# Splitting the raw pieces of each FFN's two ordinary pairs from buffers of their own, ahead of the turned tokens' copies

## The chip, the core and the metric

One NeuronCore of a Trainium2 chip runs the whole program. The metric is the device time of one execution in microseconds (us). A NeuronCore has a matrix engine (TensorE, PE in the profile, with its weight loads as PEld), a vector engine (VectorE, DVE), a scalar engine (ScalarE, ACT), a general engine (GpSimd, POOL) and a sync engine that issues transfers (SyncE, SP). PE accumulates into PSUM, which has 8 banks of 128x512 float32 here; the other engines read the banks and release them. Each engine works through its own list of instructions in order and waits at an instruction until what it needs is there.

## The reference

One layer of an encoder block on 512 tokens of width 1024: a half-step SwiGLU FFN, a token mixing stage, and a second half-step FFN, each between two RMS norms. The change touches the two FFNs:

```python
def _rmsnorm(x, g):
    xf = x.astype(jnp.float32)
    y = xf * lax.rsqrt(jnp.mean(xf * xf, axis=-1, keepdims=True) + NORM_EPS)
    return (y * g.astype(jnp.float32)).astype(x.dtype)

def _swiglu(x, w_gate, w_up, w_down):
    return (jax.nn.silu(x @ w_gate) * (x @ w_up)) @ w_down
...
    f = _swiglu(_rmsnorm(x, ffn1_pre_g[l]), ffn1_w_gate[l], ffn1_w_up[l], ffn1_w_down[l])
    x = x + 0.5 * _rmsnorm(f, ffn1_post_g[l])
...
    f = _swiglu(_rmsnorm(x, ffn2_pre_g[l]), ffn2_w_gate[l], ffn2_w_up[l], ffn2_w_down[l])
    x = x + 0.5 * _rmsnorm(f, ffn2_post_g[l])
```

D_MODEL is 1024 and D_FF is 2816, that is 22 blocks of 128 hidden features, each with a gate column block and an up column block.

## The kernel before

**Number format.** Every float32 operand of a product is split in two parts, `hi` (a rounded copy, made by ACT) and `lo` (what is left, made by DVE): `split`, lines 111 to 113. A product is then three matmuls, hi by hi, hi by lo, lo by hi (`mm3`, lines 190 to 193). So each weight piece of 128x1024 costs ACT one cast on line 112 and DVE one subtraction on line 113 before PE can use it.

**Weights.** They lie in DRAM in the order of use as pieces of 128x1024 (512 KB). `convert` (line 125) loads a piece into one of two `raw` buffers of the pool `wp` (SP, line 128) and splits it. Because there are only two such buffers, the load of the next piece waits on SP until DVE has finished the split that last read the buffer, and everything that stands behind that load on SP waits too. `fetch` converts the next piece.

**One FFN** (`ffn`, line 524) runs in these steps:

1. `first_products` (line 242): four early gate pieces, multiplied with the first 256 tokens. Between them PE transposes ("turns") the normed rows of token blocks 2 and 3 into the layout of the products: `turn_rows` calls `turned` (line 295), which puts four 128x128 transposes into a PSUM bank, twice for each token block; ACT copies the bank as `hn` hi (line 304), DVE makes the lo part (line 305). Each of the four early sums is copied to a unit `g` by ACT (line 262) and completed by DVE (line 263).
2. The turned banks of blocks 2 and 3 are kept, because after the early products `keep` (line 309) copies them once more as plain float32 into the units `whole` (eight ACT copies on line 312). With four banks for early sums and four kept ones, all 8 banks are taken until the first of these copies are done.
3. The first `STD` = 2 hidden blocks are done as ordinary pairs: `proj_into` of gate and of up, each 8 times three matmuls of 128x512. Their four pieces are numbers 4 to 7 of the FFN. Between them `combined` (line 314) builds on DVE and ACT the token combinations `sum` and `v` that the next step needs.
4. `seven` (line 399) does the other 20 pairs with seven products of 256 tokens in place of eight. Its weight blocks come from `load_blocks` (line 346): for a pair j below `EARLY` = 4 it loads four 128x512 tiles on SP (t1, t3, t4 and w11), and POOL then adds the gate or up half onto t1 and t3 by two accumulating transfers (lines 361 and 362). A pair from 4 on loads its gate piece into one of the same two `raw` buffers (line 358). The pairs 0 and 1 are loaded ahead (line 570), pair j + 2 when pair j begins (`get`). The products 5, 6, 3, 7 and 4 of the first four pairs need these blocks split, which ACT and DVE do in the order of use, among ACT's copies of results out of the banks (`up`, lines 441 and 449).
5. `down` then multiplies back to width 1024.

The tiles `x`, `raw` of the first pieces, `t1` to `t4`, `w11`, `whole`, `sum`, `v`, `g` and `h` are units of 128x512 from one pool of 54 (`up`, NUNIT), given out as they come free.

**What sets the order.** Within the marked stretches PE, ACT and DVE keep the order in which the program was written; elsewhere a scheduler at build time orders each engine's list. SP keeps the written order up to the end of FFN 1. In FFN 2 the SP list is the scheduler's. POOL keeps the written order in its marked stretches.

Of the kernel before, what the change touches and what calls it, by code (L numbers as in the profile page):

```python
# [13 lines left out]
F32R = mybir.dt.float32r  # L14
BF16 = mybir.dt.bfloat16
AF = mybir.ActivationFunctionType
# [4 lines left out]
P = 128  # L21
# [24 lines left out]
def block_kernel(ctx, tc, x, gains, weights, rpb_near, rpb_all, alibi0, alibi12, out):  # L46
# [13 lines left out]
    def unit(dt=F32, name="u"):  # L60
        return up.tile([P, 512], dt, tag="u", name=name)
# [52 lines left out]


    pieces = {}
    loads = deque()
    state = {"used": False, "next": 0, "take": 0, "stop": EARLY + 2 * STD, "ahead": lambda: None}
    ordered = []
# [2 lines left out]

    spread = {b + i for b in (3 * NF, total - 3 * NF) for i in range(SPREAD)}

    def convert(n, raw=None):
        if raw is None:
            raw = wp.tile([P, PIECE], F32, tag="raw", name="raw", bufs=2)
            nc.sync.dma_start(raw, weights[n])
        hi, lo = [wp.tile([P, PIECE], F32R, tag="w", name="w") for _ in range(2)]
        split(hi, lo, raw)  # L130
        pieces[n] = [[a[:, cs] for cs in halves] for a in (hi, lo)]
# [15 lines left out]
    def fetch():  # L147
        while state["next"] in pieces:
            state["next"] += 1
        if state["next"] < state["stop"]:  # L150
            convert(state["next"])
            state["next"] += 1
        else:
            state["ahead"]()
        for _ in range(2):
            if loads:
                loads.popleft()()
# [10 lines left out]
    def take(ahead=True):  # L168
        w = pieces.pop(state["take"])
        state["take"] += 1  # L170
        if ahead:
            fill(NPIECE - 1)
        return w
# [68 lines left out]
    def first_products(turns, early):  # L242

        w = [take(False) for _ in range(EARLY)]
        for i in range(EARLY):
            o = bank("q")
            for k0 in (0, 4):
                to = o[:, 64 * k0:64 * k0 + 256]
                parts = [cut(w[i], k * P, P) for k in range(k0, k0 + 4)]
                for j in range(4):  # L250
                    for part in parts[j]:
                        nc.tensor.matmul(to, part, hn_hi[:, k0 + j, 0:256], start=k0 + j == 0 and part is parts[j][0],
                                         stop=False, skip_group_check=True)
                for j in range(4):
                    nc.tensor.matmul(to, parts[j][0], hn_lo[:, k0 + j, 0:256], start=False, stop=j == 3,
                                     skip_group_check=True)
            if i in turns:
                turn_rows()
            if i == min(turns):
                fetch()  # L260
            g = unit(name="g")
            nc.scalar.copy(g[:, :256], o[:, :256])
            nc.vector.tensor_tensor(g[:, :256], g[:, :256], o[:, 256:], op=ALU.add)
            early.append((o, g))
        while kept:
            kept.popleft()()
        fetch()

    def sumsq(src, acc, f=1.0):

# [108 lines left out]
    def seven(use, mv, n_pairs, n0, behind, far, lead, raws, early):  # L379

        blocks = {}
        o = {}

        def get(j):
            if j < n_pairs and j not in raws:
                raws[j] = load_blocks(n0, j)  # L390
            elif j >= n_pairs:
                behind(far)

        def ready(j, i):
            if j < n_pairs:
                if j and loads:
                    loads.popleft()()
                if i == 1:
                    sums_of(raws[j])
                if j >= EARLY or i not in (1, 2):  # L400
                    blocks[j, i] = split_block(raws[j].pop(i))
            else:
                behind(lead)

        def product(j, i, key, start):
            if start:
                o[key, j] = bank(key)
            w = blocks.pop((j, i))
            acc = o[key, j][:, :256]
            for k in range(4):  # L410
                mm3(acc, w[:, k * P:(k + 1) * P], w[:, 512 + k * P:512 + (k + 1) * P], *mv[i][k],
                    start and k == 0, k == 3, skip_group_check=True)
            return acc

        res = {}
        get(0)
        get(1)
        for i in (1, 5, 2, 6, 3, 7, 4):
            ready(0, i)
        for j in range(n_pairs + 1):  # L420
            now, was = j < n_pairs, j > 0
            get(j + 2)
            if now:
                if j < EARLY:
                    o["q", j], g = early[j]
                    q = o["q", j][:, :256]
                else:
                    q = product(j, 1, "q", True)
                    g = unit(name="g")
                    nc.scalar.copy(g[:, :256], q)  # L430
                u = unit(name="up")
                res[j] = g, u
            ready(j + 1, 1)
            if was:
                q0 = product(j - 1, 7, "q", False)
                g0, u0 = res.pop(j - 1)
                nc.vector.tensor_tensor(u0[:, 256:], u0[:, 256:], q0, op=ALU.subtract)
            ready(j + 1, 5)
            if now:
                p = product(j, 5, "p", True)  # L440
                nc.scalar.copy(u[:, 256:], p)  # L441
            ready(j + 1, 2)
            if now and j >= EARLY:
                r = product(j, 2, "r", True)
                nc.vector.tensor_tensor(g[:, :256], g[:, :256], r, op=ALU.add)
            ready(j + 1, 6)
            if now:
                product(j, 6, "q", False)
                nc.scalar.copy(u[:, :256], q)
            ready(j + 1, 3)  # L450
            if was:
                product(j - 1, 4, "q", False)
                use(j - 1, g0, u0, q0)
            ready(j + 1, 7)
            if now:
                product(j, 3, "p", False)
                nc.vector.tensor_tensor(u[:, :256], p, u[:, :256], op=ALU.subtract)
            ready(j + 1, 4)
# [74 lines left out]
    def ffn(g, store, src):  # L533
        hidden = [None] * NF
        m = BLOCKS[store]
        feats = order_of(m)
        duos = [[None] * m for _ in range(2)]
        n0 = state["take"]

        def times(j, a, b):  # L540

            k = feats.index(j)
            if j < STD:
                hidden[k] = b
                nc.vector.tensor_tensor(b, a, b, op=ALU.mult)
                return
            for i in range(2):
                part = slice(i * 256, i * 256 + 256)
                if duos[i][k // 2] is None:
                    duos[i][k // 2] = unit(name="h")  # L550
                to = duos[i][k // 2][:, (k % 2) * 256:(k % 2) * 256 + 256]
                nc.vector.tensor_tensor(to, a[:, part], b[:, part], op=ALU.mult)

        def use(j, pg, pu):
            h = unit(name="h")
            nc.scalar.activation(h, pg, AF.Silu)
            times(j, pu, h)

        def use7(j, g, u, q):
            nc.scalar.activation(g[:, :256], g[:, :256], AF.Silu)  # L560
            nc.scalar.activation(g[:, 256:], q, AF.Silu)
            times(STD + j, u, g)

        raws = {}
        sums = combined()

        early = []
        first_products((0, 2) if store else (1, 2), early)
        mv = next(sums)
        for j in range(2):  # L570
            raws[j] = load_blocks(n0, j)
        for j in range(STD):
            ps = [bank(), bank()]
            for i in range(2):
                proj_into(ps[i], take(False))
                next(sums)
                if j < STD - 1:
                    fetch()
            use(j, *ps)
            if j == 0:  # L580
                ordered[-1].append(mark())
        g_post, g_pre = gain(g), None if store else gain(g + 1)
        if not store:
            bias_plan()
        after = n0 + 2 * NF
        state["stop"] = total if store else total - 3 * NF - NK

        far, lead, rest = down(m, after, duos, hidden, g_post, g_pre, store, src)
        state["next"] = state["take"] = after + 2 * m + 2
        seven(use7, mv, NF - STD, n0, lambda q: [f() for f in q.popleft()], far, lead, raws, early)  # L590
        rest()
# [1053 lines left out]
```

## Time and profile before

| | |
|---|---|
| median of three runs | 1096.55 us (1096.54 to 1097.75) |
| the profiled execution's own time | 1096.21 us |
| its span, first to last instruction | 1094.4 us |
| mean granted TensorE clock | 0.998 |
| PE idle, as far as a wait is named | 4.6, 3.5 (two waits), 1.2, 0.4 and 0.2 us |

The profile names an instruction by its line, engine, operation and the tiles it writes and reads; "idle before, releaser" says how long the engine stood before it and what ended that. The products of FFN 1 run to 346 us, those of the mixing stage from there to 747 us, those of FFN 2 from there to the end. A busy PE row is what the profile models as the matmul's own duration; the next matmul starts before it ends, so rates are read from start to start.

### The profile page before, as it was taken

How to read it: one execution, taken by the hardware profiler on the slowest of the kernel's cores; microseconds unless marked ns; L12 is line 12 of the kernel's file. 1: busy time of each engine (PE TensorE's matmuls, PEld its weight loads, DVE VectorE, ACT ScalarE, POOL GpSimd, SP SyncE). 2: the span in 40 equal slices, each digit the busy share in tenths (PEclk: the TensorE clock that was granted, in tenths of full speed). 3: DMA queues.
4: the chain of work that ended last, by engine and by line, in shares of the span. 5: the costliest groups of instructions: out<-in, count | busy, mean ns of one | idle time of the engine just before them, and what ended most of it. 6: DMA issues, size and time to landing. Idle time of an engine off the chain costs nothing.

```text
span 1094.4 us, 18389 instructions
## 1 busy us (share of the span) xinstructions
PE 1077.8 (98%) x6689; PEld 971.0 (89%) x6689; DVE 834.7 (76%) x1553; ACT 655.8 (60%) x1325; POOL 181.4 (17%) x252
## 2 busy tenths in 40 slices
PE   9999999999999999999999999999899999999997
PEld 7899999998888988888988888888799999998886
DVE  7988777778987778876477645776978777778985
ACT  6645655565784877667656641376455555565762
POOL 3212221014333000000000001142212111104301
PEclk9999999999999999999999999999999999999999
DMA  6999997569993454322132249552958777769962
GB/s 227 259 205 251 238 227 187 148 167 285 237 280 90 132 186 135 120 83 78 59 103 80 94 153 269 155 97 97 283 140 214 184 172 183 189 190 241 216 204 77
DMA packets 94573, 189.82 MB, mean 173 GB/s; under 512 B 23953, under 2 KB 26513, under 8 KB 94482
## 3 DMA queue, kind: packets, MB, share of 16 engines
q1 hardware_dynamic: 67168, 134.17, 36.9%
q0 software_dynamic: 24624, 54.01, 27.3%
q8 instruction: 52, 0.85, 0.3%
q10 hardware_dynamic: 2690, 0.46, 0.2%
q14 instruction: 39, 0.32, 0.1%
HBM read 183.58 MB, written 7.58 MB: 175 GB/s over the span
## 4 chain that ended last, share of the span: by engine, by line
PE 90%; DVE 4%; DMA 2%; ACT 2%; issue 1%; POOL 0%; SPq 0%; DVEq 0%; POOLq 0%; ACTq 0%
PE q L191 10%; PE q L193 10%; PE q L192 10%; PE ps L191 9%; PE ps L193 9%; PE ps L192 9%; PE p L191 3%; PE p L193 3%; PE p L192 3%; PE r L193 2%; PE r L192 2%; PE r L191 2%; PE c L192 2%; PE c L193 2%; PE c L191 2%; DVE w L113 1%
## 5 line engine op out<-in xcount | busy, mean ns | idle before, releaser
L113 DVE TENSOR_TENSOR w<-raw,w 128x1024 fp32r<-128x1024 f32 (+1 forms) x128 | 122.5, 957 | 76.2 <-ACT w L112 76.0
L112 ACT CAST w<-raw 128x1024 fp32r<-128x1024 f32 (+1 forms) x128 | 107.3, 839 | 88.6 <-PE ps L192 41.5
L191 PE MATMUL ps<-hn,w 128*128 128x512 f32 (+1 forms) x408 | 155.5, 381 | 3.5 <-ACT whole L312 3.5
L193 PE MATMUL ps<-hn,w 128*128 128x512 f32 (+1 forms) x408 | 153.6, 376 | 0.4 <-DVE w L113 0.2
L192 PE MATMUL ps<-hn,w 128*128 128x512 f32 (+1 forms) x408 | 153.1, 375 | 0.0
L112 ACT CAST w<-t 128x512 fp32r<-128x512 f32 x160 | 97.2, 619 | 54.5 <-DVE t L367 29.0
L113 DVE TENSOR_TENSOR w<-t,w 128x512 fp32r<-128x512 f32 x160 | 108.9, 689 | 25.8 <-ACT w L112 23.4
L191 PE MATMUL p<-v,w 128*128 128x256 f32 x320 | 90.9, 285 | 4.6 <-ACT up L441 4.6
L191 PEld LDWEIGHTS ps<-hn,w 128*128 128x128 f32 x408 | 76.9, 188 | 16.4 <-ACT whole L312 3.9
L192 PE MATMUL p<-v,w 128*128 128x256 f32 x320 | 90.9, 284 | 0.0
L191 PE MATMUL q<-v,w 128*128 128x256 f32 x320 | 90.8, 284 | 0.0
L193 PE MATMUL p<-v,w 128*128 128x256 f32 x320 | 90.8, 284 | 0.0
L192 PE MATMUL q<-v,w 128*128 128x256 f32 x320 | 90.8, 284 | 0.0
L193 PEld LDWEIGHTS ps<-hn,w 128*128 128x128 f32 x408 | 76.8, 188 | 15.6 <-DVE w L113 1.7
L193 PE MATMUL q<-v,w 128*128 128x256 f32 x320 | 90.6, 284 | 0.0
L192 PEld LDWEIGHTS ps<-hn,w 128*128 128x128 f32 x408 | 77.0, 189 | 12.5
L361 POOL DMA_DIRECT2D t<-in_weights_dram x40 | 35.0, 874 | 298.4 <-DMA t<-in_weights_dram 84.6
L193 PE MATMUL q<-hn,w 128*128 128x256 f32 x288 | 81.5, 283 | 0.0
L191 PE MATMUL q<-hn,w 128*128 128x256 f32 x288 | 81.5, 283 | 0.0
L192 PE MATMUL q<-hn,w 128*128 128x256 f32 x288 | 81.5, 283 | 0.0
L191 PE MATMUL q<-w,a 128*128 128x512 f32 x192 | 75.1, 391 | 0.4 <-DVE part L816 0.4
L192 PE MATMUL q<-w,a 128*128 128x512 f32 x192 | 74.7, 389 | 0.0
(268 smaller groups left out, 3023.3 us busy)
## 6 DMA issues: line engine op xcount, KB each, us to landing
raw<-in_weights_dram SPq DMA_DIRECT2D x98, 512.0 KB
t<-in_weights_dram SPq DMA_DIRECT2D x88, 256.0 KB
t<-in_weights_dram POOLq DMA_DIRECT2D x80, 256.0 KB, 5.7
w<-in_weights_dram SPq DMA_DIRECT2D x40, 256.0 KB
rows<-in_weights_dram SPq DMA_DIRECT2D x32, 256.0 KB
w<-in_weights_dram POOLq DMA_DIRECT2D x32, 256.0 KB, 6.1
tb<-in_weights_dram POOLq DMA_DIRECT2D x12, 512.0 KB, 8.4
rows<-in_weights_dram POOLq DMA_DIRECT2D x24, 256.0 KB, 10.8
```

The source lines that it names most:

```text
L112: nc.scalar.copy(hi, src)
L113: nc.vector.tensor_tensor(lo, src, hi.bitcast(F32), op=ALU.subtract)
L191: nc.tensor.matmul(o, sh, mh, start=start, stop=False, **kw)
L192: nc.tensor.matmul(o, sh, ml, start=False, stop=False, **kw)
L193: nc.tensor.matmul(o, sl, mh, start=False, stop=stop, **kw)
L361: nc.gpsimd.dma_start(t1, weights[gate][:, :512], accum_op=ALU.add)
```

## The change

The four pieces of the two ordinary pairs (4 to 7 of each FFN) no longer go through the two shared `raw` buffers. A new function `stage` gives each piece two units of its own and loads it as two halves of 128x512; `first_products` stages all four pieces of the FFN at its start. `convert` splits a staged piece half by half. `fetch` is called after each of the two turns (before: after the first turn, and after the `keep` copies), so the splits of the pieces 4 and 5 both stand ahead of the eight copies of line 312. `load_blocks` is called for three pairs ahead in place of two, and `get` leaves them out. In FFN 2 one small Silu activation on a 128x1 column, which brings its function table with it, is written ahead of the first products.

```diff
+    staged = {}
...
+    def stage(n):
+        staged[n] = [unit(name="raw"), unit(name="raw")]
+        for u, cs in zip(staged[n], halves):
+            nc.sync.dma_start(u, weights[n][:, cs])
+
     def convert(n, raw=None):
+        if n in staged:
+            hi, lo = [wp.tile([P, PIECE], F32R, tag="w", name="w") for _ in range(2)]
+            for u, cs in zip(staged.pop(n), halves):
+                split(hi[:, cs], lo[:, cs], u)
+            pieces[n] = [[a[:, cs] for cs in halves] for a in (hi, lo)]
+            return
         if raw is None:
...
     def first_products(turns, early):
 
         w = [take(False) for _ in range(EARLY)]
+        first = state["take"]
+        for n in range(first, first + 2 * STD):
+            stage(n)
...
             if i in turns:
                 turn_rows()
-            if i == min(turns):
                 fetch()
...
         while kept:
             kept.popleft()()
-        fetch()
...
         def get(j):
-            if j < n_pairs and j not in raws:
+            if j < n_pairs and j > 2:
                 raws[j] = load_blocks(n0, j)
...
         early = []
+        if store:
+            nc.scalar.activation(small("ms"), mhalf, AF.Silu)
         first_products((0, 2) if store else (1, 2), early)
         mv = next(sums)
-        for j in range(2):
+        for j in range(3):
             raws[j] = load_blocks(n0, j)
```

Two places show how instructions move. The first is SP's list in FFN 2, from the stores of the kept rows (`x_kept`) to the blocks of `seven`. Before (lines 128 and 358 are loads into the two shared buffers; t_8862 is the first tile of pair 2):

```order
L528 DMA x_kept<-x 128x512 x2
L128 DMA raw<-in_weights_dram 128x1024 x2
L350 DMA t_8660<-in_weights_dram 128x512
L351 DMA t_8661<-in_weights_dram 128x512
L355 DMA t_8664<-in_weights_dram 128x512
L360 DMA w_8659<-in_weights_dram 128x512
L350 DMA t_8670<-in_weights_dram 128x512
L351 DMA t_8671<-in_weights_dram 128x512
L355 DMA t_8674<-in_weights_dram 128x512
L360 DMA w_8669<-in_weights_dram 128x512
L358 DMA raw<-in_weights_dram 128x1024 x2
L350 DMA t_8862<-in_weights_dram 128x512
```

With the change, from the same place on (line 129 is `stage`, line 363 is `load_blocks`; t_8714 is the first tile of pair 2):

```order
L541 DMA x_kept<-x 128x512 x2
L129 DMA raw<-in_weights_dram 128x512 x2
L105 DMA gain_8885<-in_gains_dram 128x1024
L363 DMA t_8694<-in_weights_dram 128x512
L364 DMA t_8695<-in_weights_dram 128x512
L368 DMA t_8698<-in_weights_dram 128x512
L373 DMA w_8693<-in_weights_dram 128x512
L363 DMA t_8704<-in_weights_dram 128x512
L364 DMA t_8705<-in_weights_dram 128x512
L368 DMA t_8708<-in_weights_dram 128x512
L373 DMA w_8703<-in_weights_dram 128x512
L363 DMA t_8714<-in_weights_dram 128x512
```

The two pairs of loads into shared buffers are gone from between the blocks: pair 2's tiles now follow those of pairs 0 and 1 directly, the other six staged halves stand ahead of these rows, behind the first six `x_kept` stores, and the two gate loads of line 358 stand earlier, in the mixing stage.

The second is ACT's list at the start of FFN 2, from the squares of the last rows (line 272, then 285) to the `whole` copies. Before:

```order
L272 ACTIVATE junk,ssx<-x 128x512 x2
L304 CAST hn<-ps 128x4x128 x2
L112 CAST w<-raw 128x1024
L262 COPY g<-q 128x256 x2
L304 CAST hn<-ps 128x4x128
L560 ACT_TABLE_LOAD
L560 ACTIVATE g<-g 128x256 x2
L304 CAST hn<-ps 128x4x128
L262 COPY g<-q 128x256
L560 ACTIVATE g<-g 128x256
L262 COPY g<-q 128x256
L312 COPY whole<-ps 128x2x128 x8
```

With the change:

```order
L582 ACT_TABLE_LOAD
L582 ACTIVATE ms<-mhalf 128x1
L317 CAST hn<-ps 128x4x128 x2
L112 CAST w<-raw 128x512 x2
L276 COPY g<-q 128x256 x2
L317 CAST hn<-ps 128x4x128
L573 ACTIVATE g<-g 128x256
L317 CAST hn<-ps 128x4x128
L112 CAST w<-raw 128x512 x2
L276 COPY g<-q 128x256
L573 ACTIVATE g<-g 128x256
L276 COPY g<-q 128x256
```

The table load has moved from between the two copies of block 3's banks to ahead of block 2's copies, and the split of piece 5 (before: one cast right behind the eight copies) now stands ahead of them: the eight copies follow these rows.

## The prediction

> **What bounds the kernel now.** I read the page first, then the waits of PE, then the chain of waits through the longest of them.
>
> ```profile
> span 1094.4 us, 18389 instructions
> PE 1077.8 (98%) x6689; PEld 971.0 (89%) x6689; DVE 834.7 (76%) x1553; ACT 655.8 (60%) x1325; POOL 181.4 (17%) x252
> PE 90%; DVE 4%; DMA 2%; ACT 2%; issue 1%; POOL 0%; SPq 0%; DVEq 0%; POOLq 0%; ACTq 0%
> ```
>
> PE is busy for 98% of the span and holds 90% of the chain that ended last. This change removes no matmul, so all it can win is time in which PE stands still or runs slowly. The waits of PE and of its weight loads (who waited for whom; total us, times, longest):
>
> ```profile
> PE p L191 <- ACT up L441: 4.6, 1, 4.6
> PE ps L191 <- ACT whole L312: 3.5, 2, 2.2
> PEld ps L193 <- DVE w L113: 1.7, 4, 0.5
> ```
>
> All three stand where the diff works: two at the ends of the first products, four small ones in the ordinary pairs, one long one at the second pair of seven products in FFN 2. The chain through the long one (start, duration), and PE around it in order of time, with the granted clock of one microsecond behind it:
>
> ```profile
> 781.43 4.06 DMA t<-in_weights_dram
> 786.05 8.20 DMA t<-in_weights_dram
> 794.87 0.38 ACT up L441
> ...
> 795.29 0.39 PE L191 MATMUL p<-v,w 128*128 128x256 f32 x1 [4.55 <-ACT up L441]
> ...
> 799.00 0.32 PE L191 MATMUL q<-v,w 128*128 128x256 f32 x1
> 796.00:797.00 1.00, 1.00 (x7) 1.00 (x6) 0.96 (x2) 0.67 (x2) 0.47 (x1) 0.50 1.13 266
> ```
>
> PE waits for a copy that frees a bank. ACT is late with it because the cast of pair 2's t1 stands ahead of it in ACT's list, and that tile was loaded from 781.4 and then added to by POOL's transfer, which took 8.2 us. Behind the pause the clock column reads 0.50: the 18 matmuls from 795.29 to 799.00 took 3.71 us, where at the usual 0.12 us from start to start they take 2.16. The pause costs 4.55 + 1.55 = **6.1 us**.
>
> Why the tile was so late stands in SP's queue and in the windows (in a window's row the last two numbers are the DMA engines' busy share and GB/s):
>
> ```profile
> 757.06 10.29 SPq L128 DMA_DIRECT2D raw<-in_weights_dram  x2
> 774.87 6.46 SPq L358 DMA_DIRECT2D raw<-in_weights_dram  x2
> 763.00:765.00 2.00, 1.81 (x8) 1.52 (x9) 0.04 (x1) 2.00 (x8) 0.00 (x0) 1.00 0.00 0
> 769.00:771.00 2.00, 2.00 (x10) 1.68 (x9) 2.00 (x4) 0.00 (x0) 0.00 (x0) 1.00 1.02 384
> ```
>
> SP stood twice at loads into the two shared buffers, over 757 to 767 and 775 to 781, until DVE had split what lay in them. Meanwhile the DMA engines were idle (share 0.00 at 763), and then everything came at once.
>
> **The change, part by part.**
>
> *Pair 2's blocks in FFN 2: minus 6.1 us.* With the change the two shared loads are gone from this place of SP's list, and pair 2 follows pairs 0 and 1. Behind the last `x_kept` store (SP issues it by 752, below) stand 1 MB of staged halves and gain and 12 tiles of 256 KB, 4 MB together. At the 0.384 MB/us of the row above that is 10.5 us, to 763; if the tiles' units come free only with the last early product at 761, 3 MB end at 769. POOL's additions take 8.2 us by the chain's row for the one that met the rush: pair 2 complete by 771 to 777. ACT reaches its cast after that of pair 1's last block, behind the DVE sums, at about 782. So there are 5 us to spare or more, and both the pause and the slow clock go. What is late next is pair 3: its tiles go into units that pairs 0's sums free, at about 780 here against 783 before, and PE wants them one pair later than pair 2's, some 7 us. I take the full 6.1; bounds 0 and 6.1.
>
> *The bank at the end of the first products, FFN 2: minus 0.8 us.* ACT, DVE and PE there:
>
> ```profile
> 752.69 1.05 ACT L304 CAST hn<-ps 128x512 fp32r<-128x512 f32 x2
> 757.73 0.59 ACT L304 CAST hn<-ps 128x512 fp32r<-128x512 f32 x1 [2.50 <-PE ps L301]
> 758.33 1.28 ACT L560 ACT_TABLE_LOAD   x1
> 759.63 0.73 ACT L560 ACTIVATE g<-g 128x256 f32<-128x256 f32 x2
> 762.23 0.35 ACT L262 COPY g<-q 128x256 f32<-128x256 f32 x1
> 762.49 2.30 ACT L312 COPY whole<-ps 128x256 f32<-128x256 f32 x8
> ...
> 753.28 1.29 DVE L305 TENSOR_TENSOR hn<-ps,hn 128x512 fp32r<-128x512 f32 x2 [1.42 <-ACT hn L304]
> 754.49 1.41 DVE L292 SCALAR_TENSOR_TENSOR u<-x,rstd,gain 128x512 f32<-128x512 f32 x2
> 756.95 0.75 DVE L263 TENSOR_TENSOR g<-g,q 128x256 f32<-128x256 f32 x2
> ...
> 757.09 1.04 PE L301 MATMUL ps<-ident,u 128*128 128x128 f32 x8
> 760.35 0.64 PE L255 MATMUL q<-hn,w 128*128 128x256 f32 x4
> 763.19 0.50 PE L191 MATMUL ps<-hn,w 128*128 128x512 f32 x1 [2.20 <-ACT whole L312]
> ```
>
> PE restarts 0.70 us after the first `whole` copy begins. Taking the table load out of the chain frees 1.3 us of ACT there, the split of piece 5 put in ahead of the copies costs about 1.1 (two halves). But the load, with the small activation (0.2), now delays block 2's copies by 1.5 us, from 752.69 to 754.2, and DVE with them: the scaled rows that PE turns at 757.09 are written from 756.0 in place of 754.49, each in 0.7, so the first half is there at 756.7 and the second at 757.4, when PE needs it at about 757.4. That costs PE 0 to 0.2 us; I take 0. DVE's first early sum comes at 758.5 instead of 756.95. Then ACT: Silu from 758.9, 0.33; second copy of block 3, 0.47; piece 5, 1.1; copy, Silu, copy 0.84: `whole` begins at 761.65, PE at 762.4 instead of 763.2. It can't be earlier than 762.1, since the last early copy must wait for the product that ends at 760.99. Bounds: minus 1.1, and plus 0.2 if every step takes its row's full duration instead of its start to start.
>
> [...] Here the Silu starts 0.02 us after the load's end (758.33 + 1.28 against 759.63), so the trace shows no drain.
>
> *The same place in FFN 1: minus 0.3 us.*
>
> ```profile
> 22.39 1.05 ACT L112 CAST w<-raw 128x1024 fp32r<-128x1024 f32 x1 [3.21 <-DMA raw<-in_weights_dram]
> 25.45 0.39 ACT L262 COPY g<-q 128x256 f32<-128x256 f32 x1
> 25.70 2.33 ACT L312 COPY whole<-ps 128x256 f32<-128x256 f32 x8
> ...
> 24.47 0.64 PE L255 MATMUL q<-hn,w 128*128 128x256 f32 x4
> 26.44 0.50 PE L191 MATMUL ps<-hn,w 128*128 128x512 f32 x1 [1.33 <-ACT whole L312]
> ```
>
> ACT's 3.2 us wait for a shared buffer goes, since the halves stand on SP right behind the first loads. It looks like the prize but isn't: the last early copy can't start before PE's product ends at 25.1, that is about 25.2 instead of 25.45, and the splits of pieces 4 and 5 fit in the 3.2 us. So 0.25 to 0.3 us; bounds 0 and 0.4.
>
> *Four small waits in the ordinary pairs: minus 1.5 us.* The first of them in FFN 1, and what DVE waited for in FFN 2:
>
> ```profile
> 37.69 0.39 PE L192 MATMUL ps<-hn,w 128*128 128x512 f32 x1
> 38.14 0.50 PE L193 MATMUL ps<-hn,w 128*128 128x512 f32 x1
> 38.48 0.39 PE L191 MATMUL ps<-hn,w 128*128 128x512 f32 x1
> ...
> 765.76 1.23 DVE L113 TENSOR_TENSOR w<-raw,w 128x1024 fp32r<-128x1024 f32 x1 [2.72 <-ACT w L112]
> ```
>
> From 37.69 to 38.48 two steps took 0.79 us, where the usual step is 0.227: 0.33 lost. Four such make 1.3, the weight loads' own row says 1.7; I take 1.5. They wait for the lo halves of pieces 6 and 7, which stand behind the sums on DVE. These started only when piece 5 was split, behind the copies. Now piece 5 is split before, so the sums start when the copies end, over 2 us earlier (765.76 + 1.14 = 766.9 against 763.9 in FFN 2), more than any of the four needs. Bounds 0 and 1.7.
>
> *At no price.* Eight halves for four pieces are four more issues per FFN on SP and four more casts and subtractions, a tenth of a us each, on engines that stood idle. The gains' loads move behind pair 2's; nothing asks for them before `down`. POOL's list keeps its order. On DVE the second ordinary pair's product moves ahead of two splits: DVE may stand up to 2 us there, with pair 0's blocks 7 and 4 behind it, which PE wants after three products of 1.44 us.
>
> **The sum.** 6.1 + 0.8 + 0.3 + 1.5 = 8.7 us from the profiled execution's 1096.21 (its span 1094.4): 1087.5. The median of the runs is 0.3 above it, so I predict **1087.9 us**.
>
> **Rivals.**
> 1. *The pause moves to pair 3.* For it: its tiles still wait for units. Against it: 7 us more time, and no rush. A pause of 2 us that leaves the clock alone gives 1089.9, the full 6.1 gives 1094.0.
> 2. *The front parts don't do what they say*: DVE, which now carries the splits of pieces 4 and 5 among the turned parts, delays the bank or the lo halves as before. Then only the 6.1 remain: 1090.5.
> 3. *Slower: piece 4 is late in FFN 2.* Its halves now stand on SP behind six stores of the kept rows and need free units, while before it lay in its buffer long since.
>
> ```profile
> 732.35 13.54 SPq L528 DMA_DIRECT2D x_kept<-x  x6
> 751.23 0.98 SPq L528 DMA_DIRECT2D x_kept<-x  x2
> ```
>
> The six end at 745.9, so the halves land by about 750, and ACT wants them at 755.2. All of ACT's list stands behind that cast. Each us past 755.2 is a us for PE, and a pause as long as 4.55 adds the slow clock's 1.55; from a landing at about 764.5 the loss exceeds the other gains and 0.2%: 1099.
>
> 4. *The table load costs more where it now stands*, behind the squares. Each us beyond the 1.5 delays PE's turn at 757.09 by as much, less some 0.2 of slack. Against it: nothing stands still behind the load at 758.33. [...]
>
> **How the numbers follow.** The forecast with its bounds (1086.6 to 1089) has 0.66, rival 1 0.15, rival 2 0.10, rival 3 0.04, rival 4 0.02; 0.03 is for PE losing none of its waits' time any more, 1085. The range 1085.8 to 1092.0 leaves out rival 3, the upper part of rival 1 and that last case. A measurement of this kernel tells 0.2%, 2.2 us, from no change: faster 0.91, same (the full return of the pause, 0.05, and a piece 4 that is only a little late, 0.01) 0.06, slower 0.03.
>
> **What would show it.** Pair 2: no wait of p on `up` near 790 and a clock of 1.00 throughout. Banks: PE's waits on `whole` near 1.0 and 1.4 us. Small waits: no PEld row of ps on DVE's w. I am wrong if PE waits anew for a cast between 785 and 810, or if ACT waits for `raw` ahead of the first `whole` copy.

## The result and the profile after

The changed kernel takes **1086.41 us** (median of 4 runs, 1085.6 to 1087.04), the kernel before 1096.99 us on the same chip: a ratio of 0.9902 with a 95% interval of 0.9885 to 0.9920. The profiled execution of the changed kernel took 1087.04 us, its span 1085.3 us. Timed a second time, beside the last experiments, it took 1087.43 us against 1097.14 us: 0.9911 (0.9898 to 0.9924).

The page of the changed kernel: the span, the busy times, and the shares of the chain that ended last.

```profile
span 1085.3 us, 18420 instructions
PE 1073.0 (99%) x6689; PEld 967.6 (89%) x6689; DVE 834.2 (77%) x1561; ACT 657.1 (61%) x1334; POOL 182.2 (17%) x252
PE 93%; DVE 2%; DMA 2%; ACT 1%; issue 1%; POOL 0%; SPq 0%; DVEq 0%; POOLq 0%; ACTq 0%
```

PE's busy time fell by 4.8 us although it does the same 6689 matmuls: 1.8 us of it lies around the pause of pair 2, where they no longer run at half clock (0.50 before, 1.00 now), 2.0 us ahead of 13 us, and the rest, net, at the small waits, during which the profile counts a matmul as busy. Then PE's waits (who waited for whom; total us, times, longest):

```profile
PE ps L203 <- ACT whole L325: 2.3, 2, 1.3
PE ps L314 <- DVE u L1465: 1.2, 1, 1.2
...
PE q L203 <- DVE part L831: 0.6, 1, 0.6
PE p L203 <- ACT up L454: 0.3, 1, 0.3
```

The wait of 4.6 us is gone; the last line, 0.3 us, stands in FFN 1, near 233. The second line is new: it stands at 9.4 us, ahead of the first products, in a stretch that PE ran faster in this execution (below). Of the two waits on `whole` 2.3 us are left of 3.5, and the row of weight loads that waited for `w` on DVE (1.7 us before) has no successor. How SP, ACT and PE now stand in FFN 2 (first the row of SP's queue, then ACT, then PE; start, duration), and the clock over 790 to 792:

```profile
744.59 2.82 SPq L129 DMA_DIRECT2D raw<-in_weights_dram  x6
...
760.30 1.18 SPq L373 DMA_DIRECT2D w<-in_weights_dram  x1
767.50 0.33 SPq L363 DMA_DIRECT2D t<-in_weights_dram  x1
...
751.42 1.28 ACT L582 ACT_TABLE_LOAD   x1
752.71 0.20 ACT L582 ACTIVATE ms<-mhalf 128x1 f32<-128x1 f32 x1
...
760.26 2.31 ACT L325 COPY whole<-ps 128x256 f32<-128x256 f32 x8
...
782.91 1.66 ACT L112 CAST w<-t 128x512 fp32r<-128x512 f32 x3
...
760.98 0.50 PE L203 MATMUL ps<-hn,w 128*128 128x512 f32 x1 [1.31 <-ACT whole L325]
790.00:792.00 2.00, 2.00 (x19) 2.00 (x18) 2.00 (x5) 1.18 (x3) 0.00 (x0) 1.00 0.00 0
```

SP takes up pair 2's last tile at 760.30 (before: its first not until past 781), and pair 3's first at 767.50. The casts at 782.91, pair 2's t1 among them, wait for nothing. PE restarts 0.72 us after the first `whole` copy, and at 790 it is busy throughout at a clock of 1.00.

Both traces hold the same 6689 matmuls, so the start of one and the same matmul can be compared, and the places where the distance between the traces changes are the places where time went:

| stretch | the matmul at its end, before and after (us) | change there |
|---|---|---|
| up to the first products | 12.79 and 12.08 | -0.71 |
| bank, FFN 1 | 26.44 and 25.40 | -0.33 |
| two small waits, FFN 1, and the first product of `seven` | 52.63 and 50.71 | -0.88 |
| end of `seven`, FFN 1 | 238.09 and 236.77 | +0.60 |
| bank, FFN 2 | 763.19 and 760.98 | -0.89 |
| two small waits, FFN 2 | 781.03 and 778.12 | -0.70 |
| pair 2: pause and slow clock | 799.16 and 789.84 | -6.41 |
| last matmul | 1087.51 and 1078.36 | +0.17 |

The sum is -9.15 us. At the four small waits alone it is -0.79 us in FFN 1 and -0.81 in FFN 2; 0.1 us of the third row is the first product of `seven`, and 0.1 of the seventh is still the last small wait. Three rows, the first, the fourth and the last, are of no step of the prediction. The last is the wait on `part`, 0.6 us in place of 0.4; the experiments come back to the other two. The first is already plain from the row of a small early matmul, before and after: it takes 0.62 us in the one and 0.39 in the other.

```profile
5.72 0.62 PE L1438 MATMUL gain<-row,ones_r 1*128 1x512 f32 x1
```

```profile
5.14 0.39 PE L1453 MATMUL gain<-row,ones_r 1*128 1x512 f32 x1
```

The kernel before ran this stretch slower, at a place that the change doesn't touch. That it was the clock is inferred: the clock column reads 1.00 there in both, but the traces' record of the clock begins only at 10.6 us before and at 4.4 us after, and just there PE's steps halve: in the changed kernel from 0.43 us to 0.23 between small matmuls, in the kernel before from 0.21 to 0.11 between turns.

### The profile page after: what moved, and what is told of

Same layout as the page of the kernel before. It is cut to its first block, busy times and chain, and to the rows that moved or that the text cites. A ratio compares the mean times of both kernels' runs of the same rounds, so it can differ in the third digit from the quotient of the medians.

```text
span 1085.3 us, 18420 instructions
## 1 busy us (share of the span) xinstructions
PE 1073.0 (99%) x6689; PEld 967.6 (89%) x6689; DVE 834.2 (77%) x1561; ACT 657.1 (61%) x1334; POOL 182.2 (17%) x252
## 4 chain that ended last, share of the span: by engine, by line
PE 93%; DVE 2%; DMA 2%; ACT 1%; issue 1%; POOL 0%; SPq 0%; DVEq 0%; POOLq 0%; ACTq 0%
PE ps L203 11%; PE ps L204 11%; PE ps L205 11%; PE q L203 10%; PE q L204 10%; PE q L205 10%; PE p L203 4%; PE p L204 3%; PE p L205 3%; PE r L205 2%; PE r L204 2%; PE r L203 2%; PE c L205 2%; PE c L204 2%; PE c L203 2%; PE ps L1049 1%
## 5 line engine op out<-in xcount | busy, mean ns | idle before, releaser
L113 DVE TENSOR_TENSOR w<-raw,w 128x512 fp32r<-128x512 f32 (+1 forms) x136 | 122.9, 909 | 69.7 <-ACT w L112 69.4
L112 ACT CAST w<-raw 128x512 fp32r<-128x512 f32 (+1 forms) x136 | 107.8, 799 | 83.5 <-PE ps L204 41.9
```

What stands on the lines that cost most here:

```text
L112: nc.scalar.copy(hi, src)
L113: nc.vector.tensor_tensor(lo, src, hi.bitcast(F32), op=ALU.subtract)
```

## The experiments

Each experiment is told with its time beside runs of the kernel before on the same chip (median 1097.54 us for "two pairs ahead", "three pairs ahead, without staging", "fetch as before" and "no early table load", 1097.14 us for the others), and then by the same comparison of matmuls.

### Two pairs ahead, with the pieces staged

Edit, from the changed kernel:

```diff
-            if j < n_pairs and j > 2:
+            if j < n_pairs and j > 1:
...
-        for j in range(3):
+        for j in range(2):
```

> The changed kernel, but with two pairs' blocks loaded ahead as before, not three. Theory: the pause near 790 came from SP standing at loads into the shared buffers; with the pieces staged SP stands nowhere, and pair 2's four tiles still follow pair 1's on SP. So no wait of p on up above 0.5 us between 780 and 810, granted clock 1.00, and the time of the changed kernel: 1086.4 us, within 0.8. Rival: the third pair ahead is what removes the pause. Then a wait of p on up of 2 to 4.5 us is back at pair 2, with the slow clock behind it if it is the longer one: 1088.5 to 1092.5 us.

Measured: 1087.89 us, ratio 0.9908 (0.9891 to 0.9924), 0.7 us above the theory's upper end and 0.6 us below the rival's lower end. The trace decides. SP's queue in FFN 2 (pair 2's first tile, and its last) and PE's waits:

```profile
762.31 0.33 SPq L363 DMA_DIRECT2D t<-in_weights_dram  x1
...
765.53 0.33 SPq L373 DMA_DIRECT2D w<-in_weights_dram  x1
...
PE p L203 <- ACT up L454: 0.3, 1, 0.3
```

Pair 2's first tile goes out at 762.31, not past 781 as before the change, and there is no pause. The first 11.4 us took 2.5 us longer than in the first trace of the changed kernel (the last section says why); from there every matmul up to 1055 us keeps that distance within 0.15 us. So the third pair ahead is worth nothing here; with the pieces staged the pause is gone without it.

### Three pairs ahead, without staging

Edit, from the kernel before:

```diff
-            if j < n_pairs and j not in raws:
+            if j < n_pairs and j > 2:
...
-        for j in range(2):
+        for j in range(3):
```

> The kernel before with one part of the change: three pairs' blocks loaded ahead. The ordinary pairs' pieces still go through the two shared buffers, and fetch stands where it stood. Theory: SP still stands over about 757 to 767 at the two loads into the shared buffers, but pair 2's tiles then go out with those of pairs 0 and 1 by 774, 7 us earlier than before, and are complete by about 784 where PE wants their cast at about 790. So the pause and the slow clock go (6.4 us measured between the two traces), and the waits on whole (1.3 and 2.2) and the four small ones stay: 1090.6 us, 1089.8 to 1091.4. Rival: only the staging frees SP in time; the pause stays with 4 us or more: 1096 to 1097 us. Second rival: the rush of 12 tiles instead of 8 slows the additions, a pause of 1 to 2 us without the slow clock: 1091.6 to 1092.6.

Measured: **1100.07 us**, ratio 1.0023 (1.0011 to 1.0034): slower than before. My number was wrong by 9.5 us, and all of it lies in FFN 1, which I had left out of the expectation. SP's row of the two loads for pieces 6 and 7, in the kernel before:

```profile
26.12 4.47 SPq L128 DMA_DIRECT2D raw<-in_weights_dram  x2
```

The chain of waits in the experiment, and PE's longest wait:

```profile
30.09 13.68 DMA raw<-in_weights_dram
43.84 1.05 ACT w L112
44.94 0.79 PE ps L191
...
PE ps L191 <- ACT w L112: 7.2, 1, 7.2
```

In FFN 1 the tiles of pair 2 now stand ahead of the load of piece 6, which an ordinary pair needs before them. SP issued it at 30.09 instead of 26.12, and behind pair 2's 1 MB and POOL's additions it took 13.7 us to land, past the 35.79 at which ACT cast this piece before. PE stood 7.2 us and then ran at a clock of 0.50 up to 51.40: together 10 us. In FFN 2, where the shared loads stand ahead of the blocks, the expectation held: there the pause and the slow clock went, 6.3 us, though 0.4 us came back just ahead of them, where PE waits for a cast (799.60), and 0.7 one pair later (810.38). So the third pair ahead is not just useless; without the staged pieces in front of it, it costs more than it brings.

### Three pairs ahead in FFN 2 alone

Edit: the one above, with `3 if store else 2` pairs.

> The kernel before with three pairs' blocks loaded ahead in FFN 2 alone. Theory: in FFN 1 the third pair's 12 tiles stand ahead of pieces 6 and 7 in the transfers, which made piece 6 13.7 us on its way and PE stand 7.2 us; in FFN 2 the shared loads stand ahead of the blocks, and there the pause was gone. So here FFN 1 is as before and FFN 2 loses its pause and slow clock: 6.0 to 6.6 us less than before, 1090.4 to 1091.2 us where before is 1097.0. Rival: the pause in FFN 2 was absent only because FFN 1's delay shifted everything by 10 us against the transfers; then it is back: 1096 to 1097.

Measured: 1092.25 us, ratio 0.9955 (0.9942 to 0.9968). The rival is out: at pair 2 the trace gains 6.35 us with FFN 1 as before. But 1.7 us come back one pair later. SP's queue, the chain, and PE:

```profile
775.65 5.62 SPq L358 DMA_DIRECT2D raw<-in_weights_dram  x2
...
781.36 10.69 DMA t<-in_weights_dram
...
792.61 6.62 DMA t<-in_weights_dram
...
800.25 0.39 PE L191 MATMUL q<-v,w 128*128 128x256 f32 x1 [1.56 <-ACT up L449]
```

Here SP stands over 775.65 to 781.27 at the two loads of line 358 into the shared buffers, and now it is pair 3 that waits behind them: its t1 takes 10.69 us to land, its additions 6.62 us more, and PE waits 1.56 us. This is the prediction's first rival, the pause that moves to pair 3. With staging it doesn't come, because these two loads no longer stand there (SP issues them in the mixing stage, from 672.57): SP issues pair 3 from 767.50.

### Fetch as before

Edit, from the changed kernel:

```diff
                 turn_rows()
-                fetch()
+            if i == min(turns):
+                fetch()
...
             kept.popleft()()
+        fetch()
```

> The changed kernel, but with fetch called as before: after the first turn and again after the copies into whole, so that piece 5 is split behind them. Theory: the four small waits of the weight loads on the lo halves are back, about 0.9 us in FFN 1 and 0.7 us in FFN 2 by the two traces; of FFN 1's up to 0.6 are swallowed by waits on ACT near 235 that the faster FFN 1 met; the bank in FFN 2 comes 0 to 0.5 us earlier without the split ahead of it. In sum 0.4 to 1.2 us slower than the changed kernel: 1086.8 to 1087.6 us. Rival: the lo halves are in time also there, because the staged halves no longer wait for a shared buffer; the time is then that of the changed kernel or 0.5 us less: 1085.9 to 1086.4 us.

Measured: 1087.18 us, ratio 0.9903 (0.9889 to 0.9918). That lies within the theory's range, but it doesn't separate the two expectations, since the changed kernel itself took 1086.41 and 1087.43. The trace does: no weight load waits for a lo half in an ordinary pair, and against the first trace of the changed kernel the distance doesn't move at the four small waits (0.00 us in both FFNs). It moves by -0.13 us at FFN 2's bank, and by +0.24 and +0.45 at the first products of `seven` in FFN 1 and FFN 2 (50.95 and 786.65), where PE waits for a lo half and for a cast. On DVE, piece 5's lo halves stand behind the eight copies again, and piece 6's follow at the old place among the sums:

```profile
27.96 1.29 DVE L113 TENSOR_TENSOR w<-raw,w 128x512 fp32r<-128x512 f32 x2 [2.06 <-ACT w L112]
29.18 1.28 DVE L333 TENSOR_TENSOR sum<-whole 128x512 f32<-128x512 f32 x2
...
35.60 1.29 DVE L113 TENSOR_TENSOR w<-raw,w 128x512 fp32r<-128x512 f32 x2
```

So the rival holds in what it says of the waits: putting piece 5's split ahead of the copies is not what removed the four. What it is worth stands elsewhere, some 0.6 us net at the bank and the first products of `seven`, which no step of the prediction names. Whether the rival's own reason holds, that the halves no longer wait for a shared buffer, the next experiment tells.

### Halves alone

Edit, from the kernel before (`own` holds the numbers of the two ordinary pairs' pieces):

```diff
-        split(hi, lo, raw)
+        for cs in halves if n in own else [slice(0, PIECE)]:
+            split(hi[:, cs], lo[:, cs], raw[:, cs])
```

> The kernel before with one edit: the pieces of the two ordinary pairs are split half by half (two casts and two subtractions of 128x512 instead of one of 128x1024), out of the same shared buffers and in the same places. Theory: the four small waits went because a half's lo part is there half a subtraction (0.6 us) earlier, not because piece 5 is split ahead of the copies, since with fetch as before they did not return. So they go here as well, 1.2 to 1.6 us, and the pause of pair 2 and the waits on whole stay: 1095.4 to 1096.2 us where before is 1097.0. Rival, the prediction's own reason: the sums on DVE start only when piece 5 is split behind the copies, so the waits stay: 1097.0.

Measured: 1094.25 us, ratio 0.9972 (0.9960 to 0.9983), from 12 runs between 1091.53 and 1098.73 us, 1.2 us below the theory's range. The time scatters too far to prove a step of 1.5 us, and the pause did not stay as it was; the trace of the first products and ordinary pairs is what counts. First DVE in the kernel before, then DVE and PE here (the first matmul that needs piece 6's lo part):

```profile
36.86 1.23 DVE L113 TENSOR_TENSOR w<-raw,w 128x1024 fp32r<-128x1024 f32 x1 [0.26 <-ACT w L112]
```

```profile
35.51 1.29 DVE L113 TENSOR_TENSOR w<-raw,w 128x512 fp32r<-128x512 f32 x2
...
37.10 0.39 PE L195 MATMUL ps<-hn,w 128*128 128x512 f32 x1
```

Before, one subtraction ran from 36.86 to 38.09 and the matmul started at 38.14, as soon as it ended. Here two halves run from 35.51, the first is done by 36.2, and the matmul at 37.10 waits for nothing. At the two small waits of FFN 1 the distance to before moves by -0.79 us and at the two of FFN 2 by -0.81, the same as with the whole change. So the small waits go with the halves alone, although the pieces still come through the shared buffers: PE waited for the end of one long subtraction of which it needed only the first half. The halves help twice, for the subtraction also starts sooner: 35.51 is 0.5 us ahead of 36.86 once the 0.82 us by which this trace is ahead there are taken off. Which of the two steps suffices by itself was not tried.

The pause of FFN 2 is there, one place later and in another shape: PE waits 3.25 us for a cast (794.77) and the stretch at half clock is twice as long as before (6.84 us against 3.42). FFN 1 has two waits of its own, 0.9 us at 92.0 and 0.8 us near 235; I did not follow these up.

### No early table load

Edit, from the changed kernel: the two lines with the small Silu are left out.

> The changed kernel without the small Silu ahead of FFN 2's first products, so that the table load stands again where the first Silu of an early sum needs it. Theory: the load (1.28 us) is back in the chain of ACT between the copies of block 3's banks and the first whole copy, which now also carries piece 5's split; PE's wait on whole in FFN 2 grows from 1.3 to about 2.5, and the time by 1.2: 1087.6 us, 1087.1 to 1088.3. Rival: ACT finds 1.2 us of waiting elsewhere in that stretch and the move was worth nothing: 1086.4, within 0.4.

Measured: 1088.88 us, ratio 0.9914 (0.9898 to 0.9930). The table load back in ACT's chain (ACT, then PE):

```profile
755.20 0.59 ACT L317 CAST hn<-ps 128x512 fp32r<-128x512 f32 x1 [2.40 <-PE ps L314]
755.80 1.28 ACT L573 ACT_TABLE_LOAD   x1
757.10 0.72 ACT L573 ACTIVATE g<-g 128x256 f32<-128x256 f32 x2
...
759.76 2.31 ACT L325 COPY whole<-ps 128x256 f32<-128x256 f32 x8
...
760.48 0.50 PE L203 MATMUL ps<-hn,w 128*128 128x512 f32 x1 [2.02 <-ACT whole L325]
```

The same place of ACT in the changed kernel's first trace:

```profile
756.36 0.59 ACT L317 CAST hn<-ps 128x512 fp32r<-128x512 f32 x1 [0.90 <-PE ps L314]
757.60 0.42 ACT L573 ACTIVATE g<-g 128x256 f32<-128x256 f32 x1 [0.65 <-DVE g L277]
```

PE's wait grows from 1.31 to 2.02 us, 0.7, not 1.2. The load (1.28 us) is paid at both places; standing early it fills time in which ACT waits anyway, 2.40 - 0.90 - 0.65 = 0.85 us, less 0.2 for the small activation. So 0.7 of the 0.89 us of FFN 2's bank are the earlier table load. The medians agree in sign (2.5 us above the first time of the changed kernel, 1.5 above the second), but executions of one kernel differ by as much (the four of this one by 3.1 us), and the 0.7 rests on the trace.

### The changed kernel once more

> The changed kernel once more, unchanged, beside the others of this call, to tell what belongs to the change from what differs between executions. Theory: the first 0.7 us of the gap between the two first traces came from the clock of the first 10 us, which is granted at another moment in each execution, and the 0.6 us given back near 235 came from one transfer (ta) that took 6.1 us there and 4.6 us before. So the start of the first products varies by 1 us or more between executions of the same kernel, while everything from there to FFN 2's restart keeps within 0.3 us of the first trace but for that wait. Median 1086.0 to 1088.0 us. Rival: the change itself moves the start; the first products then start within 0.2 us of where they did (10.74 us).

Measured: 1087.43 us, span 1084.7 us. The start of its first products was 10.80 us, so this pair of traces alone would support the rival. Over all ten traces it doesn't: PE, ACT and DVE run the same instructions up to there in all of them, and the first products start at 10.63, 10.95 and 11.54 us in the three kernels built from the one before, and at 10.29, 11.03, 11.87 and 12.45 in the four others built from the changed one. That spread belongs to the execution. The second open row does too: at the end of FFN 1's `seven` this trace is 0.7 us ahead of the first one, so that of the 0.60 nothing is given back. What stands behind it (ACT; first the changed kernel's first trace, then the kernel without the early table load, which has the same instructions up to here):

```profile
232.18 1.05 ACT L112 CAST w<-ta 128x1024 fp32r<-128x1024 f32 x1 [5.17 <-DMA ta<-in_weights_dram]
```

```profile
230.05 1.05 ACT L112 CAST w<-ta 128x1024 fp32r<-128x1024 f32 x1 [3.51 <-DMA ta<-in_weights_dram]
```

ACT waits for the tile `ta`, whose load landed 6.1 us after its issue in the one and some 1.6 us sooner in the other. Where it is long, ACT's copies behind it come late for PE. Why the same load takes so different a time was not tried.

### The bank freed earlier

Edit, from the changed kernel:

```diff
                 turn_rows()
+                if i == max(turns):
+                    kept.popleft()()
                 fetch()
```

> The changed kernel with one edit more: the first of the kept banks is copied into whole right behind the last turn, ahead of piece 5's split, not behind the last early sum. Theory: PE's two waits on whole (1.0 us in FFN 1, 1.3 in FFN 2) are for that bank alone, since PE restarts 0.7 us after the first of the eight copies begins; freed earlier, the bank is there when the last early product ends and both waits go, at no cost, since the number of copies is the same: 1.8 to 2.3 us less than the changed kernel in the same call, 1084.3 us. Rival: the delayed split of piece 5 or a lo half is then late, or a wait on ACT later (FFN 1's end, ta) swallows it: less than 1 us.

Measured: **1085.14 us**, ratio 0.9890 (0.9877 to 0.9904), 2.3 us less than the changed kernel timed beside it. ACT copies the first kept bank right behind the last turn, and PE goes from the last early product into the first ordinary one without a wait:

```profile
758.35 0.65 ACT L327 COPY whole<-ps 128x256 f32<-128x256 f32 x2
758.88 1.16 ACT L112 CAST w<-raw 128x512 fp32r<-128x512 f32 x2
...
759.01 0.64 PE L270 MATMUL q<-hn,w 128*128 128x256 f32 x4
759.49 0.40 PE L203 MATMUL ps<-hn,w 128*128 128x512 f32 x1
```

Against the second trace of the changed kernel the distances move by -1.17 us at FFN 1's bank and -1.47 at FFN 2's, and 0.3 us are lost ahead of the latter, around the last turn. The wait was never for the eight copies as a whole, only for the first two. Of PE's waits above 0.3 us only two are left in this trace, the one on the first instruction and 0.5 us on `part`.

## Why the prediction was right, point by point

The forecast was 1087.9 us, from 8.7 us off the profiled 1096.21. The two timings are 1086.41, just below the bounds that it gave itself (1086.6 to 1089), and 1087.43, within them; those bounds are not the sum of the terms' own, which allow 9.3 us and so 1087.2 at the lowest. The terms against the traces:

| term | forecast | measured | shown by |
|---|---|---|---|
| (a) pair 2's blocks, pause and slow clock | -6.1 | -6.3 | traces; two pairs ahead; three ahead in FFN 2 |
| (b) bank, FFN 2 | -0.8 | -0.9 | trace; 0.7 of it the table load |
| (c) bank, FFN 1 | -0.3 | -0.3 | trace |
| (d) four small waits, both FFNs | -1.5 | -1.6 | traces; halves alone; the reason given fell by fetch as before |
| not in the sum: start, first product of `seven` in FFN 1, rest of `seven`, end | 0 | -0.7, -0.2, +0.7, +0.2 | ten traces; fetch as before; `ta`; the wait on `part` |

- **Pair 2.** The cause was as told: SP stood at loads into the two shared buffers. None of the signs named for being wrong is there. Pair 2's additions land at 774.1 and 776.2, in the 771 to 777 that was forecast, and ACT's casts of 782.91 don't wait for them. The prediction didn't say which of the two edits does it. Staging does it without the third pair ahead, which adds nothing to it.
- **Bank, FFN 2.** The prediction had `whole` begin at 761.65 and PE at 762.4. FFN 2 began 1.38 us earlier (ACT's squares at 749.92 instead of 751.30); with that the measured 760.26 and 760.98 are 761.64 and 762.36.
- **Table load.** The rival that it costs more ahead of block 2 fell: the small activation starts at 752.71, 0.01 us after the load's end, and at the old place the first Silu starts 0.02 us after it (755.80 + 1.28 against 757.10 in the kernel without the early load). ACT stands still behind the load at neither place.
- **Small waits.** The size was right and the reason wrong. The step said that the lo halves came in time because piece 5 is split ahead of the copies, so that the sums start 2 us earlier. With the old order of fetch the waits stayed away, and with halves alone they went. It is the size of the split's steps: the subtraction takes 1.23 us for a piece and 0.68 for a half, and PE needs the first half first. That the size came out all the same is no credit to the reason: it was read off the waits themselves, and any way of removing them gives it.
- **Rival 1** is a real mechanism and needs the shared loads of line 358 between pair 2 and pair 3: three pairs ahead in FFN 2 alone pays 1.7 us there. The prediction's reason against it, 7 us more time, was too weak; what excludes it is that those loads have left this place of SP's list, so that pair 3's first tile goes out at 767.50 and not at the 780 that the prediction took.
- **The gap of the medians**, 10.6 and 9.7 us in the two timings, is 0.5 to 1.4 us more than the 9.15 of the first pair of traces. The terms that were not in the sum differ between executions by about as much. One thing on record points further: the profiled execution of the kernel before, from which the forecast priced the slow clock, had a mean granted clock of 0.998, and all 30 timed with the experiments had 0.990 to 0.996 (the changed kernel's eight: 0.997 to 0.999). So the 1.55 us of slow clock were probably read from a mild case, and that the term matched in this pair of traces may in part be luck. Where those executions ran at half clock is not known, as no trace of them was kept.

## What to carry to other kernels

Here the transfers that waited for a buffer held everything behind them in SP's queue, for 10.29 and 6.46 us in FFN 2 of the kernel before, so give the loads that must wait buffers of their own before loading further ahead: loading further ahead by itself put 1 MB in front of a piece that PE needed first and cost 10 us. Where PE waits for a split or for a bank, look for the part of the work that it needs first: splitting it in halves removed 1.6 us here, and two copies of eight, moved ahead, 2.3 us. Before crediting a microsecond to an edit, compare the same instruction in both traces, and look at whether the first place where they part has anything to do with the edit.

## What the hardware showed that was not expected

What a pause cost in slow clock did not follow the length of the pause. The windows with the granted clock (third number from the right) at both ends of the slow stretch, in the kernel before (pause of 4.55 us):

```profile
795.00:796.00 1.00, 0.71 (x4) 0.71 (x5) 1.00 (x2) 0.79 (x3) 1.00 (x2) 0.83 1.08 258
...
799.00:800.00 1.00, 1.00 (x9) 1.00 (x9) 1.00 (x4) 0.03 (x1) 0.86 (x1) 0.96 1.11 264
```

with halves alone (pause of 3.25 us):

```profile
793.00:794.00 1.00, 0.00 (x0) 0.00 (x0) 0.00 (x0) 0.00 (x0) 0.00 (x0) 0.77 1.10 262
...
800.00:801.00 1.00, 1.00 (x9) 1.00 (x8) 0.72 (x2) 0.37 (x1) 0.15 (x1) 0.81 1.11 211
```

and with three pairs ahead without staging (pause of 7.2 us):

```profile
41.00:42.00 1.00, 0.00 (x0) 0.00 (x0) 0.00 (x0) 0.00 (x0) 0.00 (x0) 0.58 1.07 297
...
51.00:52.00 1.00, 1.00 (x5) 0.79 (x4) 1.00 (x2) 1.00 (x3) 0.00 (x0) 0.80 0.56 93
```

A window's mean of 0.83 between 1.00 and 0.50 says that the clock fell 0.34 us before its end, at 795.66; 0.96 says that it rose at 799.08. So the slow stretches are 3.4, 6.8 and 10.2 us long (795.66 to 799.08, 793.54 to 800.38, 41.16 to 51.40): one, two and three times 3.41. The shorter pause of 3.25 us had the longer slow stretch, of which PE lost 2.5 us (25 matmuls from 794.77 to 800.27 took 5.50 us, at the usual 0.12 us 3.0), against 1.55 us behind the pause of 4.55. Nor did the fall of the clock keep to one place of the pause: it came 0.37 us after PE had started again in the kernel before (795.29), but 1.23 us ahead of that with halves alone (794.77) and 3.78 ahead with three pairs ahead (44.94).

What the traces of the kernel before and the changed kernel record of the clock has the same step. From its first rise it stays at 1.00 for 785.07 us in the kernel before, then at 0.50 for 3.413 us and at 1.00 for 293.55, up to a fall at 1092.62, behind PE's last matmul; in the changed kernel it stays at 1.00 for 1078.61 us, up to a fall at 1083.00. In units of 3.413 us these are 230.0, 1, 86.0 and 316.0. The first rise comes 10.59 us into the one trace and 4.4 us into the other. My estimate, from these lengths alone, is that the clock changes only at whole steps of 3.413 us from its first rise. Then it matters where between two of them a pause lies, and the same kernel can pay in one execution and not in another; what makes the steps was not shown. The 12 runs of halves alone would fit that: the fastest, 1091.53 us, had a mean granted clock of 0.998, the slowest, 1098.73, one of 0.991. The wait of 2.2 us before was followed by a clock of 1.00 (758 to 766), and the execution with the wait of 2.02 us, without the early table load, had a mean of 0.999, as the changed kernel's: these two paid nothing.

The same length shows at the start of the program: with two pairs ahead the clock fell again at 7.48 us, for 6.84 us, two such steps, and the first products started 1.7 us later than in the first trace of the changed kernel (12.45 against 10.74).

```profile
7.00:8.00 1.00, 0.91 (x5) 0.67 (x6) 0.70 (x2) 0.00 (x0) 0.00 (x0) 0.74 0.82 305
8.00:10.00 2.00, 1.29 (x5) 0.60 (x4) 0.18 (x1) 1.93 (x5) 1.08 (x3) 0.50 1.04 396
...
14.00:16.00 2.00, 2.00 (x18) 2.00 (x17) 1.14 (x2) 1.97 (x6) 0.47 (x2) 0.92 1.03 388
```

So a difference of 1 to 2 us between two profiled executions of this program can lie wholly in its first 14 us, ahead of anything that an edit touched.
